# A hybrid trunk layer: second-phase blocks of 2, 3, 4, 4, 4 tiles, w_out's low words stored in the second block, sample keys in a shared pool, two FFN chunks opened together

## Chip, cores and metric

One core of a Trainium2 chip. The metric is device time in microseconds (us) of one execution, median of three runs. PE is TensorE, DVE VectorE, ACT ScalarE, POOL GpSimd, SP SyncE, whose queue issues most DMAs.

## The reference

One layer of a streaming encoder on 2048 prompt tokens (16 tiles of 128) and 128 sample tokens (8 sequences of 16, one tile that the kernel calls SMP, number 16). Cut to its skeleton:

```python
h = rmsnorm(x, norm1_g) * (1 + sc1) + sh1
proj = h @ w_in                                   # 1024 -> 3592 columns
o_a = mixer_a(proj, ...)                          # gated delta rule, 4 heads of 128
o_b = band_attention(proj, cache, rel_bias)       # 8 heads of 64; 512 past keys and its own chunk
x = x + g1 * (concat(o_a, o_b) @ w_out)           # 1024 x 1024
h = rmsnorm(x, norm2_g) * (1 + sc2) + sh2
y = x + g2 * (relu(h @ w_up) ** 2 @ w_down)       # 1024 -> 4096 -> 1024
```

The sample tokens attend to 512 cached keys and values per sequence and to their own 16. All data is float32.

## The kernel before, in words

Every large product is made of three matmuls: a float32 operand is split into a high part that TensorE takes and a low rest, and hi x hi, hi x lo and lo x hi are summed (`mm3`, L160 to L164). A weight chunk is [128, 1024] and comes through `weights` (L166): a 512 KB load into one of three `raw` tiles (L174), a cast on ACT that gives the high words (L175), and the low words as a difference on POOL (L180, recorded at L82). There are four `w` tiles. `self.keep[name]` says whether low words just made are also stored in DRAM (L183); when a chunk whose low words are stored comes again, they are loaded (L178) and POOL has nothing to do.

Phase 1 makes the projections, the delta rule and the first block's attention. Phase 2 (L1525) runs over BLOCKS2 (L34). For each block of tiles:

- `out_proj` (L1427) loads both mixers' outputs (`of`, tag "htmp", two tiles, L1434), splits them into `hT`, and multiplies by w_out in eight chunks, in the column groups 0, 1 and 2+3. In the last group a tile's residual row x is complete; `normed` makes xn (its power is on POOL), and three ticks later `load_a` transposes xn through PSUM (`psh`, L345) and scales it into "htmp" tiles, and `load_b` splits it into `hT`. What is still deferred at the end is run by `flush`.
- `ffn` (L1489) makes 32 chunks of w_up (`ffn_up`, L1467; tile psu) and after each four of them the two halves of a w_down group (psd). A block of four tiles (T = 512) makes its first chunk in two column halves, and the flush stands between them (L1472 to L1474), so that the first two tiles' matmuls run ahead of the last two tiles' transposes.
- Between FFN matmuls, `tick` draws steps from generators queued ahead of the FFN: the attention of the *next* block (`attention_gen`, 9 steps a prompt tile and 4 more) and, where that block holds SMP, `sample_gen` (L1324, 74 steps). They are paced to end at 95% of the FFN (L1544), and `drain` (L1516) runs what is left.

`sample_gen` loads the queries and new keys (`nat`, L1335), then for each of eight sequences four tiles of cached keys (`kn`, L1361), which PE transposes (psk), the cached values (KVs) and the sequence's new values (`vw`, L1377, tag "htmp"). It makes scores (psSs), a softmax, its transposes (psPs) and the value product (psos, L1405), which reads vw. nat and kn share the tag "kn", two tiles of a pool of their own.

psu, psd, out_proj's products (pso) and phase 2's transposes psh share three PSUM tiles, tag "g". Attention has other PSUM tiles.

The code gives the order of the program. A planner in the framework estimates each instruction's duration and fixes each engine's order and the tiles' places from that; on the chip each engine, and SP's queue of DMA issues, follows its order and waits on semaphores. So a load stands in SP's queue behind all that the planner put ahead of it. An instruction with nothing to wait for can be placed long before its program position: nat is loaded near 1123 us, though sample_gen is queued with the fourth block's FFN.

The low words kept: w_out and w_down in block 0, w_up in block 1 (L1535).

Of the kernel before, what the change touches and what calls it, by code (L numbers as in the profile page):

```python
# [8 lines left out]
F32 = mybir.dt.float32  # L9
# [5 lines left out]
P = 128  # L15
D = 1024
KT = 8
SEQ = 2048
NTILE = 16
SMP = 16  # L20
# [10 lines left out]
EPS = 1e-6  # L31
NEG = -1.0e30
BLOCKS1 = [[0, 1, SMP], [2, 3, 4], [5, 6, 7], [8, 9, 10], [11, 12, 13], [14, 15]]
BLOCKS2 = [[0, 1], [2, 3, 4, 5], [6, 7, 8, 9], [10, 11, 12, 13], [14, 15, SMP]]  # L34
NGRP = 4
NT2 = max(len(b) for b in BLOCKS2)
LATE = (4, 2)
# [14 lines left out]
class Trunk:  # L52
# [973 lines left out]
    def phase1(self):  # L1026
        nc, tc = self.nc, self.tc
        with ExitStack() as st:
# [43 lines left out]
            self.ap = R_("p1at")  # L1072
            self.queue(self.attention_first(BLOCKS2[0]), 1 + BH + BH // 2 * len(BLOCKS2[0]) + BH + 2, lane=2)
            self.queue(self.conv_gen(), 6, lane=1)
# [249 lines left out]
    def sample_gen(self):  # L1324

        nc, i = self.nc, self.i
        mm = nc.tensor.matmul
# [4 lines left out]
        nc.sync.dma_start(bias, self.s_bs.rearrange("h s c -> (h s) c"))  # L1332
        nats = []
        for src in (self.s_q[SMP], self.s_kn):
            nat = self.sp.tile([P, 512], F32, tag="kn", name="nat", bufs=2)  # L1335
            nc.sync.dma_start(nat, src)
            nats.append(nat)
        nc.vector.memset(qb, 0.0)
# [14 lines left out]
        for b in range(NB):  # L1353
# [4 lines left out]
            for t in range(4):  # L1358
                if t == 2:
                    yield  # L1360
                kn = self.sp.tile([P, 4, P], F32, tag="kn", name="kn", bufs=2)  # L1361
                nc.sync.dma_start(kn, i["cache_k_band"][0, b, t * P:(t + 1) * P].rearrange("p (a u) d -> p a (u d)", u=2))
                kns.append(kn)
                if t % 2:
                    yield
                    pt = self.ap2.tile([P, 1024], F32, tag="att", name="psk", bufs=2)
                    for w in range(2):
                        for p in range(4):
                            nc.tensor.transpose(pt[:, (4 * w + p) * P:(4 * w + p + 1) * P], kns[t - 1 + w][:, p], self.ident)
                    pv = pt.rearrange("p (w a t) -> p w a t", w=2, a=4)  # L1370
                    for a in range(2):
                        nc.scalar.copy(KTs[a][:, :, (t - 1) * P:(t + 1) * P].rearrange("p a (w t) -> p w a t", w=2),
                                       pv[:, :, 2 * a:2 * a + 2])
# [11 lines left out]
            ps = self.ap2.tile([P, 1024], F32, tag="att", name="psSs", bufs=2).rearrange("p (z c) -> p z c", z=2)[:, :, 0:264]  # L1385
# [78 lines left out]
            return self.o["y_sample"].rearrange("b s d -> (b s) d")  # L1464
        return self.o["y_prompt"][0, t * P:(t + 1) * P, :]

    def ffn_up(self, fi, h2, T):  # L1467
        nc = self.nc
        mm = nc.tensor.matmul
        ws = self.wslices("w_up", 0, fi * P, P, KT, KT)  # L1470
        ps = self.gp.tile([P, 512], F32, tag="g", name="psu")
        for c0, c1 in (((0, 256), (256, T)) if fi == 0 and T == 512 else ((0, T),)):  # L1472
            if c1 == T:
                self.flush()  # L1474
            for k in range(KT):
                wh, wl = ws[k]
                mm(ps[:, c0:c1], wh, h2[:, k, 0, c0:c1], start=(k == 0), stop=False)  # L1477
                mm(ps[:, c0:c1], wh, h2[:, k, 1, c0:c1], start=False, stop=False)  # L1478
                mm(ps[:, c0:c1], wl, h2[:, k, 0, c0:c1], start=False, stop=(k == KT - 1))  # L1479
        r = self.fp.tile([P, self.nt * P], F32, tag="r", name="r", bufs=1)  # L1480
        self.act(r[:, 0:T], ps[:, 0:T], AF.Relu)
        u = self.fp.tile([P, 2, self.nt * P], F32R, tag="u", name="u", bufs=NGRP + 1)
        self.act(u[:, 0, 0:T], r[:, 0:T], AF.Square)
        self.stt(ps[:, 0:T], ps[:, 0:T], 0.0, r[:, 0:T], ALU.max, ALU.mult)
        self.tt(u[:, 1, 0:T], ps[:, 0:T], u[:, 0, 0:T].bitcast(F32), ALU.subtract)
        self.tick(24 * T)
        return u

    def ffn(self, tiles, h2, x1):  # L1489
        nc = self.nc  # L1490
        n = len(tiles)
        T = n * P
        y = [self.fp.tile([P, D], F32, tag="y", name="y", bufs=self.nt) for _ in tiles]
        G, NF = NGRP, FF // P
        us = []
        for fi in range(NF + 1):
            if fi < NF:
                us.append(self.ffn_up(fi, h2, T))
            if fi == 0 or fi % G:
                continue  # L1500
            g = fi // G - 1
            for half in range(2):
                hs = slice(half * 512, (half + 1) * 512)
                ws = self.wslices("w_down", g * G, half * 512, 512, G, 2)
                for j in range(n):
                    ps = self.gp.tile([P, 512], F32, tag="g", name="psd")
                    for f in range(G):
                        self.mm3(ps, us[f][:, 0, j * P:(j + 1) * P], us[f][:, 1, j * P:(j + 1) * P], ws[f][0], ws[f][1],
                                 f == 0, f == G - 1)
                    if g == 0:  # L1510
                        nc.scalar.copy(y[j][:, hs], ps)
                    else:
                        self.tt(y[j][:, hs], y[j][:, hs], ps, ALU.add)
                    self.tick(3 * G * 512)
            us = us[G:]
        self.drain()  # L1516
        gates = {t == SMP: None for t in tiles}
        for k in gates:
            gates[k] = self.gate_tile(1, k)
        for j, t in enumerate(tiles):  # L1520
            self.tt(y[j], y[j], gates[t == SMP], ALU.mult)
            self.tt(y[j], y[j], x1[j], ALU.add)
            nc.sync.dma_start(self.y_dst(t), y[j])

    def phase2(self):  # L1525
        nc, tc = self.nc, self.tc
        with ExitStack() as st:
            P_ = lambda name, **kw: st.enter_context(tc.tile_pool(name=name, bufs=1, **kw))
            self.p2, self.hp, self.fp, self.sp = (P_(x) for x in ("p2c", "p2h", "p2f", "p2s"))
            self.nt = NT2  # L1530
            self.xnp, self.xntag, self.nxn, self.inplace = self.fp, "y", self.nt, False
            self.hT = self.p2.tile([P, KT, 2, self.nt * P], F32R, name="hT2")
            for bi, tiles in enumerate(BLOCKS2):
                n = len(tiles)
                self.keep.update(w_out=bi == 0, w_up=bi == 1, w_down=bi == 0)  # L1535
                gates = {t == SMP: None for t in tiles}
                for k in gates:
                    gates[k] = self.gate_tile(0, k)
                x1 = self.out_proj(tiles, [gates[t == SMP] for t in tiles])
                if bi + 1 < len(BLOCKS2):  # L1540
                    self.queue(*self.attention(BLOCKS2[bi + 1]))
                    if SMP in BLOCKS2[bi + 1]:
                        self.queue(self.sample_gen(), 2 + 9 * NB)
                    self.pace(0.95 * n * 24 * 2 * FF)  # L1544
                self.ffn(tiles, self.hT, x1)
# [43 lines left out]
```

## Time and profile before

| | us |
|---|---|
| median of 3 runs (3213.71 to 3215.14) | 3214.93 |
| the profiled execution | 3219.78 |
| its span, first to last instruction | 3217.7 |

| engine | busy us | share of span |
|---|---|---|
| PE | 3072.2 | 95% |
| DVE | 1765.4 | 55% |
| ACT | 1471.7 | 46% |
| POOL | 574.9 | 18% |

How to read it: an engine is busy while one of its instructions executes. Matmuls are pipelined: each shows its whole passage, so consecutive ones overlap, and the cost of one in a row of many is the distance between starts. The granted clock is a share of 2.4 GHz; 0.5 is the lower level of 1.2 GHz, and a value between means that a stretch had both. A wait is put down to the instruction that ended it. A DMA has two records, its issue by a queue and its landing; where the chain of work that ended last shows a DMA, the time is from issue to landing.

### The profile page before, as it was taken

To read this page: it belongs to the slowest core of one execution; us is meant where nothing else is said; L and a number is where in the kernel's file an instruction comes from. 1 tells how busy PE (TensorE), PEld (TensorE's weight loads), DVE (VectorE), ACT (ScalarE), POOL (GpSimd) and SP (SyncE) were. 2 spreads that over 40 slices of the span, in tenths; PEclk is the share of its full clock that TensorE was granted. 3 is DMA by queue.
4 is the path that set the end of the run, shared out by engine and by line. 5 is a ranking of instruction groups with operands and counts; after the bars stand their busy time and mean duration, and the time that the engine had idled before them with its cause. 6 is when DMAs were issued, how large, how long until landed. Compare 5 with 4: busy or idle time off the path is not lost.

```text
span 3217.7 us, 52979 instructions
## 1 busy us (share of the span) xinstructions
PE 3072.2 (95%) x19577; PEld 2720.7 (85%) x19577; DVE 1765.4 (55%) x4358; ACT 1471.7 (46%) x2803; POOL 574.9 (18%) x487
## 2 busy tenths in 40 slices
PE   6999999999989979988999999999999999998998
PEld 5998988899988978878888888888888887787997
DVE  4775777777868663777225556244556433243223
ACT  3554544555656555654334435344434433333332
POOL 3631212120212337631122110000000000000000
PEclk9999999999989989989999999999999999999999
DMA  9799897887978768885565666566675666677776
GB/s 295 232 291 292 255 295 222 258 263 240 298 244 272 227 224 265 253 289 159 177 200 182 211 232 213 179 191 200 196 258 176 213 226 225 221 245 227 255 247 196
DMA packets 630267, 751.62 MB, mean 234 GB/s; under 512 B 59808, under 2 KB 483728, under 8 KB 627960
## 3 DMA queue, kind: packets, MB, share of 16 engines
q1 hardware_dynamic: 624248, 716.78, 70.1%
q0 software_dynamic: 5760, 31.46, 2.9%
q8 instruction: 154, 2.52, 0.3%
q14 instruction: 105, 0.86, 0.1%
HBM read 635.48 MB, written 115.52 MB: 233 GB/s over the span
## 4 chain that ended last, share of the span: by engine, by line
PE 74%; DMA 14%; DVE 7%; ACT 2%; issue 2%; SPq 1%; POOL 1%; ACTq 0%; DVEq 0%; POOLq 0%
PE psu L1477 8%; PE psu L1478 7%; PE psu L1479 7%; PE psd L164 7%; PE psd L162 7%; PE psd L163 7%; PE psq L518 2%; PE psq L519 2%; PE psq L520 2%; PE psb L163 2%; PE psb L162 2%; PE psb L164 2%; PE pv L1283 2%; DMA x<-in_x_prompt_dram 2%; PE psS L1265 2%
## 5 line engine op out<-in xcount | busy, mean ns | idle before, releaser
L175 ACT CAST w<-raw 128x1024 fp32r<-128x1024 f32 (+1 forms) x528 | 551.8, 1047 | 359.2 <-PE psd L164 170.5
L1477 PE MATMUL psu<-hT,w 128*128 128x512 f32 (+2 forms) x1304 | 469.0, 361 | 4.2 <-ACT hT L104 4.2
L1478 PE MATMUL psu<-hT,w 128*128 128x512 f32 (+2 forms) x1304 | 468.3, 359 | 0.1
L1479 PE MATMUL psu<-hT,w 128*128 128x512 f32 (+2 forms) x1304 | 465.9, 357 | 0.3 <-POOL w L82 0.3
L162 PE MATMUL psd<-w,u 128*128 128x512 f32 x1088 | 431.0, 396 | 1.3 <-DVE u L82 0.8
L164 PE MATMUL psd<-w,u 128*128 128x512 f32 x1088 | 429.4, 396 | 0.0
L163 PE MATMUL psd<-w,u 128*128 128x512 f32 x1088 | 426.4, 392 | 0.0
L82 POOL TENSOR_TENSOR w<-raw,w 128x1024 fp32r<-128x1024 f32 (+1 forms) x132 | 320.1, 2434 | 325.0 <-ACT w L175 242.2
L79 DVE SCALAR_TENSOR_TENSOR psu<-psu,r 128x512 f32<-128x512 f32 (+2 forms) x160 | 98.9, 618 | 421.5 <-ACT r L92 421.4
L82 DVE TENSOR_TENSOR y<-y,psd 128x512 f32<-128x512 f32 x238 | 162.5, 685 | 246.2 <-PE psd L164 245.2
L1477 PEld LDWEIGHTS psu<-hT,w 128*128 128x128 f32 x1304 | 246.4, 189 | 38.1 <-ACT hT L104 4.9
L1479 PEld LDWEIGHTS psu<-hT,w 128*128 128x128 f32 x1304 | 246.4, 189 | 33.9 <-POOL w L82 0.9
L1478 PEld LDWEIGHTS psu<-hT,w 128*128 128x128 f32 x1304 | 246.5, 189 | 31.4 <-DVE hT L82 0.8
L92 ACT ACTIVATE r<-psu 128x512 f32<-128x512 f32 (+2 forms) x160 | 85.5, 534 | 380.0 <-issue 216.8
L164 PEld LDWEIGHTS psd<-w,u 128*128 128x128 f32 x1088 | 204.1, 188 | 46.5 <-DVE u L82 0.2
L163 PEld LDWEIGHTS psd<-w,u 128*128 128x128 f32 x1088 | 204.6, 188 | 45.6 <-issue 1.9
L162 PEld LDWEIGHTS psd<-w,u 128*128 128x128 f32 x1088 | 204.4, 188 | 44.6 <-DVE u L82 1.0
L162 PE MATMUL psb<-w,hT 128*128 128x256 f32 x816 | 237.5, 292 | 0.5 <-ACT hT L104 0.5
L163 PE MATMUL psb<-w,hT 128*128 128x256 f32 x816 | 235.4, 289 | 2.7 <-DMA w<-s_w_in 2.5
L164 PE MATMUL psb<-w,hT 128*128 128x256 f32 x816 | 235.1, 289 | 1.3 <-DVE hT L82 1.1
L518 PE MATMUL psq<-hT,w 128*128 128x384 f32 (+1 forms) x576 | 196.3, 341 | 8.3 <-ACT ba L498 8.2
L519 PE MATMUL psq<-hT,w 128*128 128x384 f32 (+1 forms) x576 | 194.7, 338 | 0.0
(316 smaller groups left out, 6501.2 us busy)
## 6 DMA issues: line engine op xcount, KB each, us to landing
raw<-in_w_up_dram SPq DMA_DIRECT2D x160, 512.0 KB
raw<-in_w_down_dram SPq DMA_DIRECT2D x160, 512.0 KB
raw<-in_w_in_dram SPq DMA_DIRECT2D x156, 512.0 KB
w<-s_w_in SPq DMA_DIRECT2D x130, 512.0 KB
w<-s_w_down SPq DMA_DIRECT2D x128, 512.0 KB
w<-s_w_up SPq DMA_DIRECT2D x96, 512.0 KB
raw<-in_w_out_dram SPq DMA_DIRECT2D x40, 512.0 KB
x<-in_x_prompt_dram SPq DMA_DIRECT2D x38, 512.0 KB
```

Source lines behind the costliest of these rows:

```text
L79: (eng or self.nc.vector).scalar_tensor_tensor(out, in0, scalar, in1, op0, op1)
L82: (eng or self.nc.vector).tensor_tensor(out, in0, in1, op)
L92: self.nc.scalar.activation(out, in_, func, **kw)
L162: mm(out, lh, rh, start=first, stop=False)
L163: mm(out, lh, rl, start=False, stop=False)
L164: mm(out, ll, rh, start=False, stop=last)
L175: nc.scalar.copy(w[:, 0, 0:n], r)
L518: mm(pc, wh, hT[:, k, 0, 0:T], start=(k == 0), stop=False)
L519: mm(pc, wh, hT[:, k, 1, 0:T], start=False, stop=False)
L1477: mm(ps[:, c0:c1], wh, h2[:, k, 0, c0:c1], start=(k == 0), stop=False)
L1478: mm(ps[:, c0:c1], wh, h2[:, k, 1, c0:c1], start=False, stop=False)
L1479: mm(ps[:, c0:c1], wl, h2[:, k, 0, c0:c1], start=False, stop=(k == KT - 1))
```

## The change

Five edits. (1) The tiles of phase 2 are cut into blocks of 2, 3, 4, 4 and 4 (the last with SMP) in place of 2, 4, 4, 4 and 3. (2) The low words of w_out are stored in block 1 and not in block 0; so block 1 makes them on POOL too, and blocks 2 to 4 load them. (3) nat and kn use the two "htmp" tiles of out_proj's pool, which vw, out_proj's `of` and load_a use already; the pool's own "kn" tiles are gone. (4) In a block of four tiles the first two w_up chunks are opened together: both chunks' matmuls on the first two tiles, then the flush, then both on the last two. (5) The rest of ffn_up moves to ffn_act, with the same operations.

```diff
-BLOCKS2 = [[0, 1], [2, 3, 4, 5], [6, 7, 8, 9], [10, 11, 12, 13], [14, 15, SMP]]
+BLOCKS2 = [[0, 1], [2, 3, 4], [5, 6, 7, 8], [9, 10, 11, 12], [13, 14, 15, SMP]]
...
-            nat = self.sp.tile([P, 512], F32, tag="kn", name="nat", bufs=2)
+            nat = self.hp.tile([P, 4, P], F32, tag="htmp", name="nat", bufs=2).rearrange("p a b -> p (a b)")
...
-                kn = self.sp.tile([P, 4, P], F32, tag="kn", name="kn", bufs=2)
+                kn = self.hp.tile([P, 4, P], F32, tag="htmp", name="kn", bufs=2)
...
-    def ffn_up(self, fi, h2, T):
+    def ffn_up(self, fis, h2, T):
...
-        ws = self.wslices("w_up", 0, fi * P, P, KT, KT)
-        ps = self.gp.tile([P, 512], F32, tag="g", name="psu")
-        for c0, c1 in (((0, 256), (256, T)) if fi == 0 and T == 512 else ((0, T),)):
+        ws = [self.wslices("w_up", 0, fi * P, P, KT, KT) for fi in fis]
+        pss = [self.gp.tile([P, 512], F32, tag="g", name="psu") for _ in fis]
+        for c0, c1 in (((0, 256), (256, T)) if fis[0] == 0 and T == 512 else ((0, T),)):
             if c1 == T:
                 self.flush()
-            for k in range(KT):
-                wh, wl = ws[k]
...
+            for w, ps in zip(ws, pss):
+                for k in range(KT):
+                    wh, wl = w[k]
...
+        return [self.ffn_act(ps, T) for ps in pss]
+
+    def ffn_act(self, ps, T):
...
-            if fi < NF:
-                us.append(self.ffn_up(fi, h2, T))
+            if made <= fi < NF:
+                new = self.ffn_up([0, 1] if fi == 0 and T == 512 else [fi], h2, T)
+                us += new
+                made += len(new)
...
-                self.keep.update(w_out=bi == 0, w_up=bi == 1, w_down=bi == 0)
+                self.keep.update(w_out=bi == 1, w_up=bi == 1, w_down=bi == 0)
```

## Rows read from the trace of the kernel before

**Rows 1.** Head of the profile page.

```profile
span 3217.7 us, 52979 instructions
```

**Rows 2.** Table of stretches: busy us and counts by engine, clock, DMA share, GB/s.

```profile
core 0: us, PE busy (x) PEld busy (x) DVE busy (x) ACT busy (x) POOL busy (x), PEclk, DMA share, GB/s
1117.00:1145.00 28.00, 18.20 (x99) 16.16 (x98) 13.64 (x23) 10.89 (x21) 10.58 (x9) 0.74 1.04 373
1145.00:1191.00 46.00, 34.70 (x222) 32.34 (x223) 35.99 (x92) 24.11 (x51) 16.56 (x13) 0.80 0.64 200
1191.00:1413.00 222.00, 216.09 (x1426) 195.04 (x1425) 139.41 (x268) 131.23 (x235) 148.55 (x75) 1.00 0.81 255
1413.00:1525.00 112.00, 92.70 (x657) 87.74 (x656) 86.01 (x208) 55.62 (x110) 16.31 (x18) 0.85 0.59 197
...
2396.00:2470.00 74.00, 66.65 (x537) 65.09 (x537) 54.53 (x136) 34.30 (x64) 4.61 (x12) 0.97 0.67 226
2470.00:2886.00 416.00, 416.00 (x2329) 334.68 (x2328) 150.97 (x329) 157.68 (x248) 3.04 (x10) 1.00 0.68 219
2886.00:2945.00 59.00, 47.11 (x334) 45.29 (x333) 30.05 (x65) 16.16 (x23) 1.94 (x3) 0.88 0.81 249
```

**Rows 3.** Timeline of PE: start us, us; steady matmuls, then one attention unit.

```profile
1455.10 0.28 PE L162 MATMUL pso<-w,hT 128*128 128x256 f32 x1
...
1456.98 0.28 PE L163 MATMUL pso<-w,hT 128*128 128x256 f32 x1
...
2594.17 0.40 PE L1477 MATMUL psu<-hT,w 128*128 128x512 f32 x1
...
2597.67 0.40 PE L1477 MATMUL psu<-hT,w 128*128 128x512 f32 x1
...
1486.11 0.60 PE L1273 MATMUL psP<-ident,sS 128*128 128x128 f32 x4
...
1487.85 0.28 PE L162 MATMUL pso<-w,hT 128*128 128x256 f32 x1
```

**Rows 4.** DMA issues from 1117 to 1145 us: count, KB each.

```profile
s_w_out<-w SPq DMA_DIRECT2D x3, 512.0 KB
...
nat<-s_q SPq DMA_DIRECT2D x1, 256.0 KB
nat<-s_kn SPq DMA_DIRECT2D x1, 256.0 KB
```

**Rows 5.** Chain that ended last (start us, us), then a wait of SP, 1191 to 1413.

```profile
1253.80 5.63 DMA raw<-in_w_down_dram
1259.51 1.06 ACT w L175
1260.63 2.43 POOL w L82
...
1405.40 8.14 DMA raw<-in_w_out_dram
...
1415.23 8.18 DMA w<-s_w_out
...
1433.30 5.23 DMA of<-s_ob
...
SPq L174 <- POOL w L82: 41.2, 18, 5.2
```

**Rows 6.** Timeline of DVE near 1165 us, and a group of the phase by lines.

```profile
1161.01 2.39 DVE L82 TENSOR_TENSOR of<-otmp 64x128 f32<-64x128 f32 x1
...
1167.37 1.78 DVE L87 TENSOR_SCALAR sS<-sS,sm 128x640 f32<-128x640 f32 x1
...
1169.72 0.23 DVE L82 TENSOR_TENSOR of<-otmp 64x128 f32<-64x128 f32 x1
...
L87 DVE TENSOR_SCALAR sS<-sS,sm 128x640 f32<-128x640 f32 x96 | 65.1, 678 | 2.2
```

**Rows 7.** A wait of PE from 2886 to 2945 (us, times, longest), and its timeline.

```profile
PE psh L345 <- DVE xn L87: 8.3, 2, 4.7
...
2936.20 1.86 PE L345 MATMUL psh<-ident,xn 128*128 128x128 f32 x8 [4.72 <-DVE xn L87]
```

**Rows 8.** A wait of SP's queue, 2566 to 2850: us, times, longest.

```profile
SPq L1435 <- PE psos L1405: 10.2, 2, 9.9
```

More of the change, by code (lines that the diff above doesn't have):

```diff
@@ L1465, in y_dst @@
         return self.o["y_prompt"][0, t * P:(t + 1) * P, :]
-    def ffn_up(self, fi, h2, T):
+    def ffn_up(self, fis, h2, T):
         nc = self.nc
         mm = nc.tensor.matmul
-        ws = self.wslices("w_up", 0, fi * P, P, KT, KT)
-        ps = self.gp.tile([P, 512], F32, tag="g", name="psu")
-        for c0, c1 in (((0, 256), (256, T)) if fi == 0 and T == 512 else ((0, T),)):
+        ws = [self.wslices("w_up", 0, fi * P, P, KT, KT) for fi in fis]
+        pss = [self.gp.tile([P, 512], F32, tag="g", name="psu") for _ in fis]
+        for c0, c1 in (((0, 256), (256, T)) if fis[0] == 0 and T == 512 else ((0, T),)):
             if c1 == T:
                 self.flush()
-            for k in range(KT):
-                wh, wl = ws[k]
-                mm(ps[:, c0:c1], wh, h2[:, k, 0, c0:c1], start=(k == 0), stop=False)
-                mm(ps[:, c0:c1], wh, h2[:, k, 1, c0:c1], start=False, stop=False)
-                mm(ps[:, c0:c1], wl, h2[:, k, 0, c0:c1], start=False, stop=(k == KT - 1))
+            for w, ps in zip(ws, pss):
+                for k in range(KT):
+                    wh, wl = w[k]
+                    mm(ps[:, c0:c1], wh, h2[:, k, 0, c0:c1], start=(k == 0), stop=False)
+                    mm(ps[:, c0:c1], wh, h2[:, k, 1, c0:c1], start=False, stop=False)
+                    mm(ps[:, c0:c1], wl, h2[:, k, 0, c0:c1], start=False, stop=(k == KT - 1))
+        return [self.ffn_act(ps, T) for ps in pss]
+    def ffn_act(self, ps, T):
+        nc = self.nc
         r = self.fp.tile([P, self.nt * P], F32, tag="r", name="r", bufs=1)
@@ L1494, in ffn @@
         G, NF = NGRP, FF // P
-        us = []
+        us, made = [], 0
         for fi in range(NF + 1):
-            if fi < NF:
-                us.append(self.ffn_up(fi, h2, T))
+            if made <= fi < NF:
+                new = self.ffn_up([0, 1] if fi == 0 and T == 512 else [fi], h2, T)
+                us += new
+                made += len(new)
             if fi == 0 or fi % G:
```

## The prediction

> **What bounds the kernel now.** I read the page first, then the table of stretches of phase 2, the matmul start times, PE's waits, the chain and the queues. The profiled execution took 3219.8 us: a span of 3217.7 [rows 1] and 2.1 around it. Its sum is made here; the median of the three timed runs, 3214.9, lies 4.9 lower.
>
> Phase 2 begins near 1117. In the long FFN stretches PE never stands still: 416.00 busy of 416 in block 3, at granted clock 1.00, so 2.4 GHz [rows 2]. There the time is matmul work, and the change leaves the sum of that work alone. Block sizes are 2, 4, 4, 4, 3 before and 2, 3, 4, 4, 4 after, so the same count of each kind of matmul. A column costs the same at any width: 16 starts of 256 columns take 1.88 us (0.1175 each, 0.459 ns a column), 15 starts of 512 take 3.50 (0.233 each, 0.456 ns) [rows 3]. Attention does the same (head, tile) units, and its key windows sum to 6+8+8+6 = 28 tiles before, 5+8+8+7 = 28 after.
>
> What can move is the time lost where one block hands to the next: PE idle, plus (1 - clock) x busy for stretches partly at 1.2 GHz. From the table [rows 2]: into block 0 (T0), (28-18.20) + (46-34.70) idle and 0.26x18.20 + 0.20x34.70 clock = 32.7 us; into block 1 (T1), 19.3 + 0.15x92.70 = 33.2; T3, 7.4 + 0.03x66.65 = 9.4, and T2 much the same; T4, 11.9 + 0.12x47.11 = 17.5. FFN 0 loses 5.9, FFN 3 nothing. T0 and T1 are the odd ones.
>
> **The change, part by part.**
>
> *T0.* In 1117 to 1145 the DMA engines are saturated: share 1.04, 373 GB/s, PE 18.20 busy of 28 [rows 2]. Three stores of w_out's low words and two 256 KB sample loads (nat) are issued there [rows 4], 1.57 + 0.52 MB; both go elsewhere. The key window of the attention started there is 5 tiles for 6: two heads, 0.26 MB. 2.35 MB / 373 GB/s = 6.3 us. Two stores issued just before it still drain inside it, and three come later. Ends: all eight, 4.98 MB / 373 = 13 us gained; and 0, if the second half sets the end, where DVE is busy 35.99 of 46 [rows 2]. I take **-7**, nearest to what the window itself shows. SP also loses its waits for POOL ahead of those stores.
>
> *FFN 0.* Tile 5's attention goes to FFN 1. One unit of five key tiles takes PE 1.74 us (1486.11 to 1487.85) [rows 3]; eight heads are 14, and query preparation makes it some 16. That is only a gain here if weights can come faster. Per chunk PE now spends 216.09 / 64 = 3.4 us; it would want 200 / 64 = 3.1. The supply is a ring of three raw tiles: landing (5.63 in one piece of the chain), cast 1.06, POOL difference 2.43 [rows 5], 9.1 us or 3.0 a chunk; with the longest raw landing of these rows, 8.14, it is 11.6 or 3.9. SP already waits 41.2 us for POOL before raw loads [rows 5]. So between 0 and all 16 us come back as idle. I take **+4**, near the first landing, because that one lies in the same stretch.
>
> *T1.* Its chain is nearly all DMA landings: a raw w_out chunk 8.14, w_out's low words 8.18, the attention output's load into out_proj 5.23 [rows 5]. The attention of tiles 2 to 5 had not finished in so short an FFN. Three tiles have 12/17 of that work (3+4+5 of 3+4+5+5 key tiles), and the low words no longer come by DMA. Nearest row for a three-tile hand-over without that tail: T4 of before, 17.5 us. Going all the way there is -15.7; a tail remains, so I take -12. Against it, POOL now makes eight differences here. They cost PE nothing if their cover, the out_proj matmuls, holds. But while POOL runs one, DVE is stretched: an `of` addition takes 2.39 us against 0.23, a scaling of sS 1.78 against a mean of 0.68 [rows 6]. About 1.5 us each, 12 us of DVE, of which perhaps two fall where attention's tail is serial: +3. T1 together **-9**; ends -16 and +7. The eight stores (4.2 MB) replace as many loads, but wait in SP's queue for POOL; x, gate and weight loads stand behind them. That is in the upper end.
>
> The Trainium skill (Perfetto Trace Analysis, "Optimizing Scalar/DVE Operations") says that GpSimd and VectorE share an SBUF read port, which a two-port VectorE operation locks, so moving work between them may not help. The trace agrees for these operations, with the 2.39 us above. By that rule alone the eight differences would be no free exchange for eight loads; what that would make is the second rival.
>
> *FFN 1* has three tiles for four of attention, less PE time per weight chunk, and POOL and the stores of w_up as before. PE was busy 97% in FFN 0 under a harder load [rows 2], so **+2**, ends 0 and +8.
>
> *T2, T3: the pair of chunks.* Before, 24 matmuls of 256 columns (2.8 us) ran ahead of the third and fourth tile's transposes; now 48 (5.6 us). The new part covers at most 2.8 us a block. It holds two of the three PSUM tiles that the transposes share, so four transposes groups go through one. No row shows that; two groups of another tile took 1.86 us with an evacuation between them [rows 7], so two more, strictly one after the other, cost some 2 to 3 us a block. Other attention work lies ready there. **-2** for both, ends -6 and +6. The second chunk's weights must stand 2.8 us earlier; the ring runs further ahead than that.
>
> *T4.* The last block has four tiles and gets the split and the pair. PE waits 8.3 us there in two waits for a normalised tile (xn). The longer, 4.72, sits after the final out_proj matmul [rows 7], and 5.6 us of up-matmuls now run in it; the other meets one more tile's 48 matmuls. From 17.5 down to T3's 9.4: **-8**; ends -14 and +2, since no attention fills this one.
>
> *FFN 3: late sample keys.* Keys (32 loads) and nat share two tiles with the sample values (vw) and with out_proj's inputs. Before, a key's load waited for earlier keys' transposes alone; now the second key of a sequence also waits for the previous sequence's value product (psos), with weight loads behind it in SP's queue. An `of` load already waited 9.9 us for psos [rows 8], in a stretch where PE idles 0 [rows 2]: the weights queued ahead cover such a wait. **+1**; ends 0 and +42 (eight sequences by one landing of 5.23).
>
> The tail after the last matmul keeps its form: 0. Freed SBUF is not used.
>
> Sum: -7 + 4 - 9 + 2 - 2 - 8 + 1 = **-19 us**, 3219.8 to 3200.8 profiled, so 3214.9 to **3196** as a median.
>
> **Rivals.**
> 1. *More of it works.* T0 -13, FFN 0 0, T1 -16, T2 and T3 -6, T4 -14, the rest 0: -49, 3166. For it: T0's and T1's losses are 66 us together. Against: DVE fills T0's second half.
> 2. *The POOL differences sit on T1's path.* 8 x 2.43 = 19.4 us of stretched DVE in place of 3: -19 + 16 = -3, 3212, no change. It needs DVE to be what PE waits for through all of T1, as it is at both ends of T1; in the middle PE works through out_proj. The Trainium skill's sentence above is the reason to give it a chance.
> 3. *Weights set FFN 0.* The 16 us stay as idle: +12 more, and with T0 hidden behind DVE, +7: -19 + 19 = 0, 3215, no change. The chain through FFN 0 speaks for it, PE's 97% against.
> 4. *Sample keys hold SP's queue: slower.* Eight sequences that each lose a landing are 42 us, less the 1 counted: -19 + 41 = +22, 3237. For it: the order of loads is fixed, and 105 steps now share the FFN that 96 shared. It decides when a wait for psos lasts longer than the weights queued ahead (three raw tiles at 24 x 0.233 = 5.6 us each, 17 us). Against: the longest seen is 9.9, and it cost nothing.
> 5. *The order of instructions comes out otherwise.* Each engine's order is fixed by a planner that estimates durations; the pair may be placed behind the transposes, or late in it. Then T2 to T4 give nothing: -9, 3206. This lies inside my forecast's range.
>
> **How the numbers follow.** A measurement of this kernel can tell about 0.2%, 6.4 us. My forecast's case (-6.5 to -35) gets 0.60, rival 5 in it; rival 1, 0.16; rival 2, 0.07; rival 3, 0.07; rival 4, 0.10. Faster 0.60 + 0.16 = 0.76, same 0.14, slower 0.10. The range 3170 to 3214 reaches almost to rival 1 and over rival 2; it leaves out half of rival 3, rival 4 and the far end of rival 1, under 0.2 in all.
>
> **What would show it.** Right: no w_out store before block 1; DMA below saturation sooner in T0; T1's loss near 24, without s_w_out loads in its chain; the wait for xn at T4 shorter; FFN stretches still full. Wrong: SP waits for psos beside PE idle in FFN 3; PE idle behind POOL in FFN 0 or T1; longer waits for hT after the pair; T1's attention tail still there.

## The result, and the profile after

**3193.1 us** (median of 10 runs, 3174.9 to 3201.9) against 3214.4 (10 runs) of the kernel before: ratio **0.9923, 95% interval 0.9905 to 0.9941**. The forecast was 3196 (3170 to 3214). The profiled execution of after took 3191.7 us, 28 less than that of before; its stretches are read here, the head of its page first.

```profile
span 3190.0 us, 53098 instructions
```

The table of stretches of after, with the columns of [rows 2], cut at the same events: the two halves of the hand-over into block 0 (T0), FFN 0, T1, FFN 1, T2, T3, FFN 3 and T4.

```profile
1112.00:1140.00 28.00, 20.73 (x144) 19.40 (x143) 17.63 (x33) 10.74 (x21) 11.79 (x9) 0.82 0.85 296
1140.00:1173.00 33.00, 25.48 (x165) 23.03 (x165) 26.52 (x78) 21.59 (x45) 14.77 (x13) 0.85 0.60 175
1173.00:1388.00 215.00, 209.28 (x1365) 188.81 (x1364) 123.23 (x237) 124.46 (x217) 153.53 (x80) 0.99 0.84 264
1388.00:1493.00 105.00, 88.79 (x591) 84.78 (x590) 81.57 (x179) 52.79 (x100) 30.80 (x23) 0.89 0.68 226
1493.00:1783.00 290.00, 290.00 (x1574) 264.08 (x1573) 142.97 (x276) 138.07 (x228) 70.16 (x43) 1.00 0.78 253
1783.00:1864.00 81.00, 74.19 (x601) 72.44 (x600) 58.66 (x150) 38.71 (x75) 3.71 (x9) 0.98 0.66 221
2260.00:2332.00 72.00, 67.88 (x563) 67.27 (x562) 53.66 (x135) 34.77 (x64) 3.60 (x9) 0.97 0.67 228
2332.00:2761.00 429.00, 427.96 (x2455) 347.94 (x2454) 172.56 (x396) 176.56 (x291) 4.16 (x13) 1.00 0.69 219
2761.00:2837.00 76.00, 65.26 (x496) 63.04 (x495) 42.11 (x89) 20.09 (x31) 2.64 (x4) 0.91 0.69 211
```

Three things are to be seen. T0's first half is no longer saturated: DMA share 0.85 for 1.04, 8.3 MB moved for 10.4, and PE is busy 20.73 of 28 for 18.20. FFN 1 is full and FFN 3 idles 1.0 of 429. T1 and T4 still lose much: T4 idles 10.7 of 76 at clock 0.91, though it was to come down to half of its 17.5.

To compare kernels, the prediction's measure (PE idle plus (1 - clock) x busy, called the loss of a stretch) was taken from such a table for every kernel, T0 from phase 2's first out_proj matmul to its first up-matmul, the other hand-overs from the block's first out_proj matmul to 20 us after its first up-matmul. A few cuts lie a few us beside those of [rows 2], so before reads 32.4 at T0 where the prediction had 32.7. The last column is phase 2's own length, the span less the start of its first out_proj matmul.

| kernel | T0 | FFN 0 | T1 | T2 | T3 | FFN 3 | T4 | phase 2 |
|---|---|---|---|---|---|---|---|---|
| before | 32.4 | 5.9 | 32.0 | 7.5 | 10.1 | 0 | 17.4 | 2099.5 |
| after | 22.2 | 7.8 | 26.0 | 8.3 | 6.2 | 1.0 | 16.6 | 2078.4 |
| new blocks alone | 29.2 | 12.7 | 17.3 | 5.9 | 9.6 | 2.7 | 9.9 | 2078.2 |
| late w_out stores alone | 26.6 | 14.8 | 29.1 | 4.8 | 7.9 | 0 | 17.2 | 2090.3 |
| late keys alone | 30.1 | 8.1 | 25.6 | 7.2 | 5.8 | 0 | 19.6 | 2088.6 |
| pair alone | 29.8 | 4.9 | 29.8 | 4.6 | 11.8 | 4.2 | 20.9 | 2095.9 |
| after, old blocks | 24.7 | 6.3 | 32.2 | 4.7 | 12.4 | 0 | 20.0 | 2090.1 |
| after, early w_out stores | 25.4 | 15.9 | 16.5 | 11.4 | 7.0 | 0.7 | 16.6 | 2080.9 |
| after, early keys | 26.1 | 5.5 | 20.0 | 8.4 | 7.6 | 0.2 | 11.2 | 2071.1 |
| after, no pair | 18.7 | 9.3 | 24.6 | 6.1 | 9.7 | 2.8 | 12.2 | 2073.8 |
| blocks and late stores only | 23.1 | 11.1 | 17.5 | 7.3 | 9.8 | 0.4 | 12.2 | 2075.7 |
| after, w_out stored in block 2 | 20.9 | 9.9 | 20.1 | 11.6 | 7.2 | 0.4 | 13.3 | 2070.4 |
| after, w_out never stored | 17.7 | 8.6 | 19.2 | 6.7 | 8.5 | 0.1 | 15.4 | 2067.4 |
| w_out in block 2, early keys | 25.7 | 8.9 | 19.9 | 11.7 | 7.0 | 0.7 | 12.0 | 2076.0 |

From before to after the columns change by -10.2, +1.9, -6.0, +0.8, -3.9, +1.0 and -0.8, and FFN 1 by -0.2: -17.4. Phase 2 itself is 21.1 shorter; a clock given to two digits does not resolve the difference. In a long FFN stretch one hundredth of the clock is 2 to 4 us, so changes of that size in the FFN columns say nothing; PE's idle time alone says more there. The other 6.6 of the span lie in phase 1, whose instructions the change leaves alone and which stand in the same order in both. Phase 1 ended between 1109.9 and 1122.5 in these fourteen executions (1109.9 to 1120.4 in the four taken on one chip), so those 6.6 are no part of the change.

### The profile page after: what moved, and what is told of

Read it like the earlier page. It is cut to its first block, busy times and chain, and to the rows that moved or that the text cites. A ratio compares the mean times of both kernels' runs of the same rounds, so it can differ in the third digit from the quotient of the medians.

```text
span 3190.0 us, 53098 instructions
## 1 busy us (share of the span) xinstructions
PE 3060.4 (96%) x19649; PEld 2717.8 (85%) x19649; DVE 1768.1 (55%) x4358; ACT 1471.8 (46%) x2803; POOL 593.5 (19%) x495
## 5 line engine op out<-in xcount | busy, mean ns | idle before, releaser
L82 POOL TENSOR_TENSOR w<-raw,w 128x1024 fp32r<-128x1024 f32 (+1 forms) x140 | 338.3, 2428 | 269.5 <-ACT w L175 184.5
L1479 PEld LDWEIGHTS psu<-hT,w 128*128 128x128 f32 x1328 | 251.1, 190 | 36.2 <-ACT hT L104 5.3
L1481 PEld LDWEIGHTS psu<-hT,w 128*128 128x128 f32 x1328 | 251.4, 189 | 32.8 <-DMA w<-s_w_up 1.0
L1480 PEld LDWEIGHTS psu<-hT,w 128*128 128x128 f32 x1328 | 251.7, 190 | 30.5 <-issue 0.8
```

What stands on the lines that cost most here:

```text
L82: (eng or self.nc.vector).tensor_tensor(out, in0, in1, op)
```

## The experiments

Every kernel was timed over several rounds beside the kernel before. The medians of before were 3213.3 (first four), 3215.2 (next four), 3215.4 (next three) and 3213.7 (last). A median moves by about 0.2% within its interval, so the table above, and differences between groups of its rows, say more of single parts. One row is one execution.

**New blocks alone** (before with this line):

```
+BLOCKS2 = [[0, 1], [2, 3, 4], [5, 6, 7, 8], [9, 10, 11, 12], [13, 14, 15, SMP]]
```

> Of the kernel before, with the blocks of 2, 3, 4, 4, 4 tiles alone. Theory A (the gains are separate: DMA relief at the first hand-over from the late w_out stores, the shorter attention tail at the second from the blocks): -6 to -10 us, T1 loses 30 in place of 33, T0 is left near its 33. Rival B (the blocks carry all of it): -19 or more, T0 shortened too. Rival C (the late stores carry all of it): within 4 us of before.

Measured: 3195.5 us, ratio 0.9948 (0.9928 to 0.9968). T1 falls from 32.0 to 17.3 and T4 from 17.4 to 9.9; FFN 0 rises from 5.9 to 12.7. Theory A and rival C fall; rival B comes nearest (-17.8 for its -19), but T0 is hardly shortened (29.2). The blocks carry most of the change's gain.

**Late w_out stores alone** (before with this line):

```
-                self.keep.update(w_out=bi == 0, w_up=bi == 1, w_down=bi == 0)
+                self.keep.update(w_out=bi == 1, w_up=bi == 1, w_down=bi == 0)
```

> Of the kernel before, with w_out's low words stored in block 1 alone. Theory A: -6 to -10 us at T0, and T1 1 to 3 us worse, because POOL makes eight more differences there: -5 to -8 in all. Rival B: within 4 us. Rival C: -15 or more. If POOL's differences sit on T1's path (third theory): T1 loses 8 to 16 us more and the sum is slower by 0 to 8.

Measured: 3209.7, ratio 0.9987 (0.9972 to 1.0002). T0 falls by 5.8 and T1 by 2.9, while FFN 0 rises by 8.9. By itself it is worth 0.3% at most, as rival B had it; the third theory falls, since T1 loses no more than before.

**Late keys alone** (the two tiles moved into htmp's pool):

```
-                kn = self.sp.tile([P, 4, P], F32, tag="kn", name="kn", bufs=2)
+                kn = self.hp.tile([P, 4, P], F32, tag="htmp", name="kn", bufs=2)
```

> Of the kernel before, with nat and kn in the shared tiles alone. Theory A: -1 to +2 us, of which nat's 0.5 MB leaves T0 (-1.4 us) and the waits for psos in FFN 3 are covered. If the keys hold SP's queue: slower by 10 us or more, with PE idle in FFN 3.

Measured: 3211.0, ratio 0.9989 (0.9975 to 1.0003). FFN 3 stays at 0. T1 reads 25.6 for 32.0, though this edit puts nothing there; kernels with one and the same order of matmuls in T1 differ by as much (17.5 to 26.0, in the table).

**The pair alone** (`ffn_up` for a list of chunks, `[0, 1]` first):

```
-                us.append(self.ffn_up(fi, h2, T))
+                new = self.ffn_up([0, 1] if fi == 0 and T == 512 else [fi], h2, T)
```

> Of the kernel before, with the two up-chunks opened together alone (blocks 1 to 3 have four tiles there). Theory A: three hand-overs, -1 us each, -3 to 0. If two held PSUM tiles cost more than the cover gives: +3 to +9, seen as transposes (psh) that go one group at a time, with waits for htmp between them.

Measured: 3212.8, ratio 1.0002 (0.9987 to 1.0017): nothing.

**After with the old blocks:**

```
+BLOCKS2 = [[0, 1], [2, 3, 4, 5], [6, 7, 8, 9], [10, 11, 12, 13], [14, 15, SMP]]
```

> The changed kernel with the old blocks 2, 4, 4, 4, 3. If the parts add up (blocks alone -17 us, the three others -7 together): 3205 to 3209, T1's loss 29 to 34, T4's 18 to 20. If the blocks are needed for the others to pay: 3211 to 3217.

Measured: 3200.3, ratio 0.9951 (0.9934 to 0.9968), faster than either reading had it. T0 keeps its gain (24.7); T1 (32.2) and T4 (20.0) lose theirs. Its phase 1 ended at 1109.9, the earliest of all, so its span flatters it: phase 2, 2090.1, is 9.4 shorter than before's and 11.7 longer than after's.

**After with w_out's low words stored in block 0:**

```
-                self.keep.update(w_out=bi == 1, w_up=bi == 1, w_down=bi == 0)
+                self.keep.update(w_out=bi == 0, w_up=bi == 1, w_down=bi == 0)
```

> The changed kernel with w_out's low words stored in block 0 again. If the late stores cost in T1 what they give in T0 (POOL's differences or the queue of stores at the second hand-over): T1 falls from a loss of 30 to about 19, as with the blocks alone, T0 rises from 25 to 31, and the total stays within 5 us of the changed kernel. If they are a clear gain: 4 to 8 us slower than the changed kernel, T1 still 30.

Measured: 3200.4, ratio 0.9943 (0.9921 to 0.9964). Its table of stretches: T0's first half, FFN 0 and T1.

```profile
1118.00:1146.00 28.00, 17.52 (x111) 15.68 (x112) 16.48 (x29) 10.54 (x21) 11.29 (x9) 0.82 1.01 361
1182.00:1406.00 224.00, 210.17 (x1361) 187.97 (x1362) 120.64 (x238) 124.01 (x217) 149.01 (x78) 0.99 0.80 257
1406.00:1500.00 94.00, 80.68 (x594) 78.01 (x593) 72.57 (x173) 52.98 (x101) 15.79 (x16) 0.96 0.73 247
```

With the stores back the DMA engines are saturated again (share 1.01, 361 GB/s) and PE falls to 17.52 of 28, although attention's key windows are those of after. So the stores, and not the smaller key window, filled T0's first half. The same 28 us hold 361 to 373 GB/s in all five kernels with stores in block 0 and 296 to 334 in the nine without. FFN 0 idles 13.8 us where after idles 5.7. T1 is the other way round, 94 us for 105, PE idle 13.3 for 16.2, clock 0.96 for 0.89. So T1 came out as the first reading had it and the total, some 7 us above after's, as the second.

**After with the sample keys in their own pool:**

```
-                kn = self.hp.tile([P, 4, P], F32, tag="htmp", name="kn", bufs=2)
+                kn = self.sp.tile([P, 4, P], F32, tag="kn", name="kn", bufs=2)
```

> The changed kernel with nat and kn in their own pool. If the shared tiles cost nothing: within 3 us, FFN 3 at 428 us as in the changed kernel, T0 1 to 2 us longer (nat back in its DMA window). If they delay FFN 3 or the last block's out_proj inputs: 4 us or more faster, in F3 or T4.

Measured: 3193.1, ratio 0.9929 (0.9908 to 0.9950), the same as after. T0 reads 26.1 for 22.2 and T4 11.2 for 16.6. The longer SP waits of after in the last 321 us of FFN 3 show why the late keys cost next to nothing there:

```profile
SPq L178 <- PE psu L1481: 71.2, 19, 7.0
SPq L178 <- PE psd L164: 48.7, 16, 8.9
...
SPq L1375 <- PE psos L1405: 17.0, 6, 4.8
SPq L1362 <- PE psk L1369: 16.2, 10, 6.6
```

SP mostly waits to refill a weight tile that PE is still reading (71.2 and 48.7 us), that is, it runs ahead. Its longest wait for the sample attention's output is 4.8 us, and PE idles 1.0 us in all of FFN 3.

**After without the pair:**

```
-                new = self.ffn_up([0, 1] if fi == 0 and T == 512 else [fi], h2, T)
+                new = self.ffn_up([fi], h2, T)
```

> The changed kernel without the pair: one up-chunk ahead of the flush. If the pair costs at the last hand-over (one PSUM tile left for four groups of transposes): T4's loss falls from 17 to about 12, as with the blocks alone, and the kernel is 2 to 6 us faster than the changed one. If it is a gain there: 2 to 5 us slower, with a wait of 3 us or more for xn before the last transposes.

Measured: 3198.6, ratio 0.9946 (0.9928 to 0.9963). Phase 2 is 4.6 shorter than after's in the profiled execution while the median is 5.5 higher, so the pair is not resolved. T4 reads 12.2 for 16.6, as the first reading had it, the median goes the way of the second.

**Blocks and late stores only** (early keys and no pair, the edits of the two experiments above together):

> The kernel after without two of its four parts: the sample keys go back to their own pool and the pair of chunks is undone; the new blocks and the late storing of w_out's low words stay. Theory (late keys and pair each cost time at the last hand-over once both are there, and win nothing elsewhere): the last hand-over loses the 4 to 5 us that the x_sample load costs, the third one gains back what the pair had cut (up to 4 us), sum 0 to -5 us against the kernel after, 3188 to 3194 us, ratio 0.991 to 0.9925 to the kernel before. Rival (parts need one another, as undoing any one of them cost up to 7 us except the keys): 3198 to 3205 us.

Measured: 3194.2, ratio 0.9940 (0.9925 to 0.9955): the theory's 3188 to 3194 is met at its edge, its ratio of 0.991 to 0.9925 is not, and the rival's 3198 and more falls. Two of the four parts make the whole gain, within what can be told.

**After with w_out stored in block 2** (block 1 makes the differences and stores nothing):

```
-                self.keep.update(w_out=bi == 1, w_up=bi == 1, w_down=bi == 0)
+                self.keep.update(w_out=bi == 2, w_up=bi == 1, w_down=bi == 0)
```

> The kernel after with w_out's low words stored in the third block (bi == 2) in place of the second. The hand-over into block 1 then has the POOL differences of the kernel after but not its eight stores; the hand-over into block 2 has both. Theory (POOL's differences stretch DVE on the path of attention's tail into block 1): block 1's hand-over loses as much as in the kernel after, and block 2's gets up to 10 us longer; 3196 to 3205 us. Rival (the eight stores in SP's queue hold up x and weight loads): block 1's hand-over falls by some 10 us to that of the version with block-0 stores, and block 2's rises by as much; 3190 to 3197 us.

Measured: 3191.7, ratio 0.9929 (0.9907 to 0.9951). From its table of stretches, T1 and FFN 1:

```profile
1399.00:1485.00 86.00, 71.67 (x501) 69.28 (x500) 62.62 (x129) 39.61 (x72) 29.63 (x18) 0.92 0.59 188
1485.00:1785.00 300.00, 300.00 (x1661) 273.76 (x1661) 162.22 (x326) 151.16 (x257) 76.00 (x50) 1.00 0.77 250
```

T1 is 19 us shorter than after's, but FFN 1 is 10 longer. Counted along PE's order, 387 matmuls stand between block 1's first out_proj and first up-matmul here, 483 in after: 96 matmuls of attention went over into FFN 1, where PE is full anyway. T1's loss, 20.1 against 26.0, tells more than its length, but the three kernels that share after's order of matmuls in T1 read 24.6, 20.0 and 17.5. The differences do reach VectorE, though. First two operations of after's DVE at the head of T1, then two of this kernel's with the wait of its PE that follows (timelines: start us, us).

```profile
1389.74 1.21 DVE L82 TENSOR_TENSOR y<-y,gate 128x1024 f32<-128x1024 f32 x1
1390.99 3.30 DVE L82 TENSOR_TENSOR y<-y,x 128x1024 f32<-128x1024 f32 x1
```

```profile
1400.49 3.41 DVE L82 TENSOR_TENSOR y<-y,gate 128x1024 f32<-128x1024 f32 x1
...
1405.79 3.21 DVE L82 TENSOR_TENSOR y<-y,gate 128x1024 f32<-128x1024 f32 x1
...
1410.85 0.58 PE L162 MATMUL pso<-w,hT 128*128 128x256 f32 x1 [4.30 <-DVE x L82]
```

POOL's differences run from 1400.30 for 2.52 us and from 1405.56 for 2.35 in this kernel, from 1390.18 for 3.02 in after: just while those operations last. Where none runs, in the version with early stores, all four such operations at this place take 1.22 or 1.23 us, and PE has no such wait. An operation that had begun before a difference kept its length, and the difference took longer: in after the first one above (1.21 us) and the 3.02 us of POOL that began 0.44 us into it. Out_proj's wait for x at this place is 4.30, 3.44 and 4.31 us in the three kernels that make the differences and store nothing in block 1, and 2.05, 1.52, 0 and 0 in the four that store them. Which meetings of an operation and a difference bring that wait is not shown: the versions that store have a stretched operation there too, two of them without the wait. Both readings miss at T1, which fell by 5.9 us where the theory had 0 and the rival 10; T2 rose by 3.3, and the total lies in the rival's 3190 to 3197.

**After with w_out never stored** (each block makes the eight differences):

```
+                self.keep.update(w_out=False, w_up=bi == 1, w_down=bi == 0)
```

> The kernel after with w_out's low words never stored: every block makes the eight differences on POOL, none stores or loads them. Theory (POOL differences are what costs in a hand-over): each of the hand-overs into blocks 1 to 4 pays some 5 to 10 us, less at the last one, where no attention waits; 3200 to 3225 us. Rival (the stores and loads are what costs, and POOL is free): all hand-overs get shorter, 3180 to 3192 us.

Measured: 3196.4, ratio 0.9942 (0.9922 to 0.9962). Neither reading takes it: the hand-overs do not each pay 5 to 10 us, nor does the total come down. T1 reads 19.2, T2 6.7, T3 8.5, T4 15.4.

**Stores in block 2 and early keys together:**

> The kernel after with two edits: w_out's low words stored in the third block, the sample keys back in their own pool. It is the second look at the hand-over into block 1 without the eight stores, and the best candidate of the single edits put together. Theory (the stores, not POOL's differences, make that hand-over long, and the late keys with the pair make the x_sample load late at the last one): out_proj's start to the first up-matmul into block 1 near 67 to 70 us against 85 in the kernel after, the last hand-over some 4 us shorter, in all 3 to 8 us under the kernel after: 3183 to 3191 us, ratio 0.990 to 0.992. Rival (one execution's hand-over is chance, since the three versions without the stores or without the keys took the same total time within 3 us): 3190 to 3198 us, and the hand-over into block 1 anywhere between 67 and 90 us.

Measured: 3194.6, ratio 0.9945 (0.9919 to 0.9970). T1 repeats itself (19.9; 67 us from out_proj's start to the first up-matmul, as the theory had it), but the total stays where the rival put it. None of the versions beats after by more than the measurement can tell: after, the blocks alone, and the five versions with early keys, with blocks and late stores only, and with w_out stored in block 2 or never lie between 3191.7 and 3196.4.

## Why the prediction was right, and where its steps were off

The sign, the size (-21.2 for -19) and the place were right: what the change moved lies in the hand-overs of phase 2, and FFN 1 and FFN 3 stayed full. That the total came within some 2 us is luck in part. In the profiled execution T4 missed its part by 7.2 us and T1 by 3.0; T0, FFN 0, FFN 1, T2 and T3 gave 3.2, 2.1, 2.2 and 1.1 more than forecast and made up for most of it. One step failed, T4; FFN 0 came near its size for another reason.

**T0, -7: right.** One execution gave -10.2. Over all rows the nine kernels with later stores, or none, average 22.9, the five with stores in block 0 29.4: -6.5. The mechanism is the one written: in the first half 2.1 MB less moved (2.35 predicted), below saturation, and with the stores back it was saturated again. The lower end, that the second half sets the end, did not hold; that half also got shorter (33 for 46 us). Those averages mix in the keys. Taken at equal blocks and keys, moving the stores gives -4.2 to -5.5 in each of four comparisons (their 1.57 MB at 373 GB/s are 4.2 us), and moving the keys at equal stores and blocks -1.0 to -5.1, mostly more than the 1.4 us of nat's 0.52 MB. The readings scatter: four kernels with one and the same order of instructions in T0 read 17.7 to 22.2.

**FFN 0, +4: the size within its bounds, the reason not seen.** The +1.9 is one hundredth of the clock; PE idles 5.7 us for 5.9. So no idle time came back, and waits for weights, the reason given, are 1.8 us for 0.3. The seven kernels with the new blocks and w_out not stored in block 0 average 8.7. With new blocks and early stores FFN 0 loses 12.7 and 15.9, but the late stores alone lose 14.8 with the old blocks, so it does not hang on the stores alone. Nor do weights set FFN 0 there, as the third rival had it: of the 13.8 us that PE idles in the version with early stores 4.3 end with a weight's cast or difference, of the 10.6 with the blocks alone 2.4; the others are mostly single waits for attention's and the FFN's own steps on VectorE and ScalarE. What decides FFN 0's idle time stays open.

**T1, -9 (-12 and +3): the mechanism right, the execution an unlucky one.** The tail that the prediction saw is gone. Block 1's four loads of attention output were issued 19 to 35 us after out_proj's first matmul in before (the first of them, at 1433.30, is in [rows 5]); after's three were issued 13 and 6 us ahead of that matmul and 3.5 us behind it (timelines: before's PE, then after's PE and SP):

```profile
1413.91 0.36 PE L162 MATMUL pso<-w,hT 128*128 128x256 f32 x1
```

```profile
1387.81 0.28 PE L162 MATMUL pso<-w,hT 128*128 128x256 f32 x1
...
1391.28 0.32 SPq L1435 DMA_DIRECT2D of<-s_ob  x1
```

What T1 still loses in after is mostly the next block's attention, drawn in between: 11.0 of its 16.2 us of idle time are waits of attention's matmuls.

Three kernels with old blocks and w_out stored in block 0 average 29.1 at T1. New blocks with low words loaded as before read 17.3 and 16.5: -12.2 for the predicted -12. With the differences and no stores in T1, 20.1, 19.2 and 19.9: +2.8 for the predicted +3, though 87 fewer matmuls stand in T1 there, so the 2.8 is not the differences' price alone. With the differences and the stores, the four kernels average 22.0 (26.0, 20.0, 24.6, 17.5, with the same order of matmuls in T1); that the stores add to it is not resolved in such a spread. The sum to 22.0 is -7.1; the -6.0 of the profiled execution comes from the highest of the four. The second rival falls: no kernel with the differences is 16 us above 16.9, and the three without stores lie some 3 us above it. The sentence of the Trainium skill (Perfetto Trace Analysis, "Optimizing Scalar/DVE Operations") that moving work between VectorE and GpSimd may not help agrees with the trace as to the stretch (1.22 to 3.30 us).

**FFN 1, +2:** nothing; full at 290 of 290. **T2 and T3, -2:** -3.1 in the profiled execution, T2 up 0.8 and T3 down 3.9. The pair is hardly the reason. With the new blocks T3 averages 7.3 in the six kernels with the pair and 9.7 in the three without, but T2 9.7 and 6.4, of which three of the six have w_out's differences there as well. What one gains the other gives back; with the old blocks T2 and T3 even changed roles.

**T4, -8: the step that failed,** -0.8 in the profiled execution. The prediction took away one wait and set T4 equal to T3 (9.4). That wait went: the two waits for a normalised tile, 8.3 us [rows 7], are one of 1.2, and the blocks do that without the pair (1.4). But other waits grew by 6.4 us in its place, and the clock stayed low. In before idle time made 11.9 of T4's loss and the clock 5.5; in after 10.7 and 5.9 (clock 0.91); with the blocks alone 8.6 and 1.3 (0.98). PE's waits at T4, one line of before and then after's:

```profile
PE pso L162 <- DVE x L82: 2.0, 1, 2.0
```

```profile
PE pso L162 <- DVE x L82: 5.2, 2, 4.8
PE psh L345 <- ACT htmp L92: 1.9, 1, 1.9
PE psh L345 <- DVE htmp L82: 1.3, 1, 1.3
PE psh L345 <- DVE xn L87: 1.2, 1, 1.2
```

The first is out_proj waiting for its PSUM to be drained into x. That DVE addition waits 7.7 us for a load of x, issued at 2766.72 and landed 13.05 us later, while the DMA engines moved 342 GB/s at a share of 1.03 (2757 to 2782). SP issues these loads in turn with the stores of block 3's outputs, the last of them for the sample tile (the chain, then timelines of SP and DVE; PE's wait ends at 2780.35):

```profile
2766.72 13.05 DMA x<-in_x_prompt_dram
...
2769.17 0.34 SPq L1531 DMA_DIRECT2D out_y_prompt_dram<-y  x1
2770.09 0.33 SPq L1444 DMA_DIRECT2D x<-in_x_sample_dram  x1
...
2779.87 0.42 DVE L82 TENSOR_TENSOR x<-pso,x 128x256 f32<-128x256 f32 x1 [7.71 <-DMA x<-in_x_prompt_dram]
```

The wait is not new with four tiles in the last block, but longer: 2.8 to 5.2 us in the nine kernels with the new blocks, 1.8 to 2.8 in the five with the old. That the stores make the load late is not shown; before issues its loads in turn with stores too, and VectorE has no wait for them there. The other two are the transposes in the single PSUM tile that the pair leaves, which the prediction priced (2 to 3 us) and then set against T2 and T3 only:

```profile
2824.44 0.60 PE L345 MATMUL psh<-ident,xn 128*128 128x128 f32 x4
2826.97 0.66 PE L345 MATMUL psh<-ident,xn 128*128 128x128 f32 x4 [1.93 <-ACT htmp L92]
2828.95 1.09 PE L345 MATMUL psh<-ident,xn 128*128 128x128 f32 x4 [1.32 <-DVE htmp L82]
```

At T2 and T3 attention's matmuls can lie between; here none are left. In all six kernels that have the pair and four last tiles T4 shows these two waits (2.7 to 3.3 us together), in the three without the pair neither; those wait 2.2 to 3.4 us for hT ahead of their up-matmuls instead, so at T4 the pair swaps one wait for another. The four kernels with late keys and pair average 15.5 at T4, the other five with the new blocks 11.5. Much of the difference is granted clock (0.91 to 0.93 in the four, 0.93 to 0.98 in the five), and the version with the pair and stores in block 2 reads 13.3, one with early keys 12.0: that the keys add to it is not shown. The blocks by themselves gave -7.5 there (9.9), near the -8, in the one execution read.

**FFN 3, +1:** 1.0; the fourth rival falls with it. **The first rival,** more of it works, is not what happened: of its -49, T0 came near, T1 and T4 did not.

The four parts tried singly sum to -17.8 for the blocks, and -3.6, -2.3 and -0.5 for the rest: -24 against -21. The three together without the blocks, however, gave -14.8 (interval -10 to -21), and of the 17.7 that this version's profiled span is shorter, 8.3 lie in phase 1, which it leaves alone. What each small part is worth by itself stays open below some 5 us.

## What to carry to other kernels

Where the same work is handed from block to block, count what each hand-over loses and move the block that has too much attention left; then look for the waits that take the place of the one removed, above all in the last block. A transfer taken out of a saturated stretch returned about its bytes at the measured rate here (4.2 to 5.5 us for 4.2), but the place it moves to may pay: some 3 us of T1's loss went with the differences. Price a buffer that one edit takes away at every place where the edit acts, above all where no other work covers it.

## What the runs showed of the hardware that was not expected

The same phase 1, instruction for instruction, ended between 1109.9 and 1122.5 us in fourteen executions, each of one core. That scatter is over half of what the change gained, and phase 2's own length is the better measure of it.

A two-input VectorE operation of 128x1024 float32 took 3.21 to 3.41 us beside a POOL difference of the same shape (2.35 to 3.02 us), and 1.22 without: some 2.0 to 2.2 us longer, most of the POOL instruction's length. Begun before the difference, it kept its 1.21 us, and POOL took 3.02 for 2.35 to 2.52.

TensorE's granted clock in the same stretch, with the same order of instructions on every engine, differed by execution. The whole of T0 in the versions without stores and with stores in block 2, from the tables of stretches of these two:

```profile
1114.00:1172.00 58.00, 44.26 (x307) 40.44 (x307) 43.37 (x108) 32.97 (x65) 27.71 (x23) 0.91 0.77 248
```

```profile
1122.00:1182.00 60.00, 48.26 (x305) 44.11 (x306) 44.67 (x108) 33.09 (x66) 27.86 (x22) 0.81 0.74 238
```

PE idles less in the second, 11.7 us for 13.7, yet the first had 1.2 GHz for about a fifth of the stretch (0.91) and the second for nearly two fifths (0.81): 0.09 x 44.26 = 4.0 us lost against 0.19 x 48.26 = 9.2. The 5.2 between them are a quarter of the change's gain.
